# Row sums of squares of four SSD blocks made earlier, and the last head pair's loads re-ordered, in a hybrid attention and SSD layer

## The chip, the cores and the metric

The kernel runs on one core of a Trainium2 chip. The time is that of one execution in device microseconds. The kernel before took 2189.46 us, the median of three runs from 2188.48 to 2193.33 us.

## The reference

For 2048 tokens of width 1024 the layer computes a projection, two branches, and one output product.

```
proj = x @ w_in                                   # q, k, v, z_att, z_ssm, xbc, dt
o_d, l_d = dilated_window_attention(q, k, v)      # for dilation d = 1, 4, 16; l_d is the log of the exponentials' sum
y_att = sum_d softmax_d(l_d) * o_d                # 16 heads of 64
y_att = rms_norm(y_att * silu(z_att))
y = ssd_chunked(conv_silu(xbc), dt, ...) + d_skip * xs
y_ssm = rms_norm(y * silu(z_ssm))
out = concat(y_att, y_ssm) @ w_out
x = layer_norm(alpha * x + out)
```

`rms_norm(u)` divides each token's row of 1024 by the root of its mean square. The kernel multiplies the un-normed rows by `w_out` (the gain is folded into the weight) and scales the product by the reciprocal root afterwards, so the sum of squares of a row is needed only when its product is added to the result.

## The kernel before

Everything is fp32, but large products are made of three float32r products: high times high, high times low, low times high. The program has three stretches.

**Projections and SSD.** `proj` makes 52 column tiles of the projection, each of 96 products of 128x512 (L111 to L113). While the last 20 tiles run, `ssd(n, g)` works on 16 blocks n of 128 tokens and two groups g of heads. It writes `y * silu(z)` of a block, its operand for the output product, to DRAM as `d_us` and, for the first four blocks, also split into high and low as `d_uh`. The order in this stretch is made by a scheduler from its own estimates.

**Attention.** Eight pairs of heads, pr = 0 to 7, one after the other. A pair has 24 steps `(d, qd, half)`: dilation 0 to 2, four quarters, two halves. In each step TensorE makes the scores (L528), DVE adds the bias table and takes a minimum (L536), ACT makes the exponentials (L544), TensorE transposes them (L557), DVE copies them out (L559) and TensorE multiplies them by v (L577) two to three steps later. From here on the order on TensorE, DVE, ACT and POOL is the order in which the code is written; only the order on SP, which issues most DMAs, is the scheduler's.

When the last step of a pair is done, its minima and sums (`st`) are transposed, written to DRAM (`d_st`, L605), read back in another layout (`cm`, L611), turned into the softmax weights over the three dilations (`weights`, L618 to L628), written (`d_wd`, L629) and read back broadcast over partitions (`wb`, six loads of 512 KB, L642). `combine` then weights and sums the three dilations' results `num` and multiplies by `silu(z)`. For pairs 0 to 6 this runs on POOL during the next pair, `weights` at the steps (0,3,0) and (0,3,1), `combine` at (1,0,0), (1,1,0), (1,3,0) and (2,2,0), and the result goes to DRAM as `d_ua` (L660). For pair 7 there is no next pair: it runs on DVE within the output stretch, its three `num` are first multiplied by `silu(z)` (`gate`, L782), and its result stays on the chip in four tiles, here called `u7` (L649).

**Output.** `product(n, br)` makes 48 products of 128x512 for block n and branch br (1 is SSD, 0 is attention): two halves `hf` of 24, each over eight weight tiles e with three products. The order is (0,1) (1,1) (2,1) (3,1), then (0,0) (1,0) (2,0) (3,0), then both branches of each block from 4 on. The operand is split by ACT (L707) and DVE (L708); for the SSD branch of blocks 0 to 3 the split is loaded from `d_uh` instead (`fetch_parts`). The eight weight tiles of the SSD branch, W[8] to W[15], are loaded by POOL during pair 7 into tiles that attention has done with, those of the attention branch, W[0] to W[7], in the output stretch, as `num`, `qp`, `v` and `wb` come free.

The sum of squares: `fetch_raw` loads the unsplit operand, `squares` squares it (ACT, L712) and sums over the eight slices (DVE `TENSOR_REDUCE`, L714), and TensorE sums over partitions by a product with a column of ones (L743), which stands in TensorE's order **between the two halves of the same block's product**. `add` takes the reciprocal root (L750, L751) and adds the scaled product to the result (L755).

The prediction's steps are in `ssd` (from L340), `weights` and `combine` (L613, L631), `fetch_parts` (L684) to `add` (L747), `gate` (L780) and the two loops from L790.

Of the kernel before, what the change touches and what calls it, by code (L numbers as in the profile page):

```python
# [9 lines left out]
F32 = mybir.dt.float32  # L10
F32R = mybir.dt.float32r
AF = mybir.ActivationFunctionType
# [16 lines left out]
def hybrid_layer(ctx, tc, xT, xc, w52, wv, convw, convb, dtb, alog, dskp, gcol, wout,  # L29
# [37 lines left out]
    nc.gpsimd.memset(epst, EPS)  # L67
    gc = consts.tile([128, 16], F32, name="gc")
    def evac(i, o, a):
        if i % 2:  # L70
            nc.vector.tensor_copy(o, a)
        else:
            nc.scalar.copy(o, a)


    with ExitStack() as c1:
# [263 lines left out]
        def ssd(n, g):  # L340
# [71 lines left out]
            if n < 4:  # L412
# [4 lines left out]
                for p, t in enumerate((yh, yl)):  # L417
                    nc.sync.dma_start(d_uh[g][n][:, p], v4(t.bitcast(F32)))

        units = [(n, g) for n in range(16) for g in range(2)]  # L420
        jobs = []
# [17 lines left out]
    with ExitStack() as c2:  # L439
# [251 lines left out]

        def fetch_raw(n, br):
            u = raw[n, br] = row().rearrange("p (c t) -> p c t", t=128)
            if br:
                for g in range(2):
                    (nc.gpsimd if n < 2 else nc.sync).dma_start(u[:, 4 * g:4 * g + 4], d_us[g][n])
            else:
                nc.sync.dma_start(u[:, 0:7], d_ua[n])
# [10 lines left out]

        def squares(n, br):  # L710
            u = raw.pop((n, br))
# [8 lines left out]

        raw, sr = {}, {}
        UT = ["num", "num", "qp"]
        banks = [("S", psS), ("S", psS), ("S", psS), ("S", psS), ("T", psT), ("T", psT)]

        def product(n, br):
# [4 lines left out]
            for hf in range(2):  # L730
# [9 lines left out]
                pss.append(ps)  # L740
                if hf == 0:
                    pn = psN.tile([128, 512], F32, name="N")
                    nc.tensor.matmul(pn[:, 0:1], sr.pop((n, br)), one, start=True, stop=True)  # L743
            free.append(t)
            return pss, pn

        def add(n, br, pss, pn):  # L747

            r = small[:, 8 * n + br:8 * n + br + 1]
            nc.scalar.activation(r, pn[:, 0:1], AF.Sqrt, bias=epst, scale=1.0 / D)  # L750
            nc.vector.reciprocal(r, r)  # L751
# [27 lines left out]

        def gate(d, eng):  # L780
            num = f2(pairs[7]["num"][d])
            eng.tensor_tensor(num, num, zt7, op=OP.mult)  # L782

# [6 lines left out]
        with tc.manual_schedule(engines={E.PE, E.DVE, E.Activation, E.Pool}):  # L790
            for i in range(len(todo) + TA + 1):
# [16 lines left out]
                if i > TA:  # L808
# [7 lines left out]
                    at = d, qd, half  # L816
                    if pr and at in ((0, 3, 0), (0, 3, 1)):
                        weights(pairs[pr - 1], half)
                    step = ((1, 0, 0), (1, 1, 0), (1, 3, 0), (2, 2, 0))
                    if pr and at in step:  # L820
                        combine(pairs[pr - 1], step.index(at))
                    if pr < 7:
# [4 lines left out]
                        if (qd, half) == (3, 1) and d < 2:  # L827
                            load_dil(pairs[pr + 1], d)
                    elif at == (1, 0, 0):
                        for e, name in ((8, "kh_0"), (9, "kl_0"), (10, "qh"), (11, "ql"), (12, "v")):  # L830
                            load_w(e, name)
                    elif at == (1, 1, 0):
                        zt7 = big("num", F32)
                        nc.gpsimd.dma_start(zt7, d_za[7])
                    elif at == (1, 3, 0):
                        for e, name in ((13, "qp"), (14, "qp")):
                            load_w(e, name)
                        fetch_parts(0, 1)
                        gate(0, nc.gpsimd)
                    elif at == (1, 3, 1):  # L840
                        load_w(15, "v")
                    elif at == (2, 2, 0):
                        fetch_parts(1, 1)
                    if pr and at == (0, 3, 1):
                        load_dil(pairs[pr], 2)
            A = pairs[7]
            small = stp.tile([128, 192], F32, name="st")
            os_ += [big("kh_1", F32), big("kl_1", F32)]
            fetch_raw(0, 1)
            squares(0, 1)  # L850
            residual(0)
            fetch_raw(1, 1)
            residual(1)
            fetch_parts(2, 1)
            fetch_raw(2, 1)
            order = [(n, 1) for n in range(4)] + [(n, 0) for n in range(4)]
            order += [(n, br) for n in range(4, 16) for br in (1, 0)]
            for i, (n, br) in enumerate(order):
                ps = product(n, br)
                if i == 0:  # L860
                    weights(A, 0)
                    weights(A, 1)
                    gate(1, nc.vector)
                    gate(2, nc.vector)
                if i == 1:
                    fetch_parts(3, 1)
                    fetch_raw(3, 1)
                    for d in range(3):
# [9 lines left out]
                if 2 <= i < len(order) - 2:  # L878
                    fetch_parts(*order[i + 2])
                    fetch_raw(*order[i + 2])  # L880
                    if order[i + 2][1] and order[i + 2][0] >= 4:
                        residual(order[i + 2][0])
                if i + 1 < len(order):
# [5 lines left out]
                if i == 2:  # L889
                    split(0, 0, slice(0, 7))  # L890
                add(n, br, *ps)
                if br == 0:
# [69 lines left out]
```

## Time and profile before

| | |
|---|---|
| median of three runs | 2189.46 us |
| profiled execution | 2193.83 us, of it 2192.0 us span |
| TensorE busy | 2138.5 us, 98% |
| DVE, ACT, POOL busy | 53%, 39%, 38% |
| granted TensorE clock, mean | 0.984 of full speed |
| chain that ended last | TensorE 89%, DMA 4%, DVE 4%, ACT 2% |

TensorE is busy nearly all the time. The profile's slices of 54.8 us show where it is not: the first slice, then two slices (33 and 34, about 1754 to 1863 us) with 7 and 6 tenths, and the last. The two slices in the middle are the passage from attention to the output stretch. In the same two slices the granted clock shows 8 tenths, and the DMA engines move 360 and 276 GB/s, among the most in the program. In such a kernel an edit changes the time if it changes what TensorE does, or how long it stands still at those places.

### The profile page before, as it was taken

The numbers are of one execution on the slowest core, as the hardware profiler recorded it, in microseconds if no ns is written. First come the engines' busy times: TensorE is split into PE (matmuls) and PEld (weight loads), VectorE is DVE, ScalarE is ACT, GpSimd is POOL, SyncE is SP. The second block draws the span as 40 slices with busy tenths as digits, with TensorE's granted clock in tenths as the row PEclk, the third lists the DMA queues.
The fourth block names the chain that finished last, engine by engine and source line by source line (L and its number), as shares of the span: only waits on it lengthen the run. The fifth ranks groups of instructions, "written<-read, shape, count | busy, mean of one in ns | idle before, by whom it ended". The sixth has DMA issues, their size and how long they took to land.

```text
span 2192.0 us, 37071 instructions
## 1 busy us (share of the span) xinstructions
PE 2138.5 (98%) x13968; PEld 1784.6 (81%) x13968; DVE 1166.2 (53%) x2941; ACT 847.8 (39%) x2289; POOL 838.8 (38%) x589
## 2 busy tenths in 40 slices
PE   8999999999999999999999999999999976999998
PEld 8999888888888888888888878888878865888886
DVE  4000255555223555554544258888888845655655
ACT  4101122223112333232345368887888841222221
POOL 3101010102442455555555321776666670322322
PEclk9999999999999999999999979999999988999999
DMA  8644222224786656555543542777876799232220
GB/s 281 182 133 139 70 78 71 77 71 148 249 262 208 206 194 198 178 190 177 171 157 129 195 148 76 228 219 223 241 216 184 208 360 276 99 104 83 93 84 29
DMA packets 213955, 363.66 MB, mean 166 GB/s; under 512 B 37776, under 2 KB 125968, under 8 KB 203536
## 3 DMA queue, kind: packets, MB, share of 16 engines
q1 hardware_dynamic: 197408, 278.45, 41.8%
q0 software_dynamic: 16368, 82.84, 10.6%
q8 instruction: 110, 1.80, 0.3%
q14 instruction: 69, 0.57, 0.1%
HBM read 226.62 MB, written 134.61 MB: 165 GB/s over the span
## 4 chain that ended last, share of the span: by engine, by line
PE 89%; DMA 4%; DVE 4%; ACT 2%; SPq 1%; issue 1%; POOL 0%; DVEq 0%; POOLq 0%; ACTq 0%
PE pp L112 14%; PE pp L111 14%; PE pp L113 14%; PE N L577 6%; PE T L557 6%; PE S L528 6%; PE S L737 3%; PE S L739 3%; PE S L738 3%; PE pp L155 2%; PE pp L156 2%; PE pp L154 2%; PE T L737 2%; PE T L738 2%; PE T L739 2%; PE ss L386 1%
## 5 line engine op out<-in xcount | busy, mean ns | idle before, releaser
L111 PE MATMUL pp<-xh,whi 128*128 128x512 f32 x1408 | 550.3, 391 | 0.0
L112 PE MATMUL pp<-xl,whi 128*128 128x512 f32 x1408 | 549.6, 390 | 0.0
L113 PE MATMUL pp<-xh,wlo 128*128 128x512 f32 x1408 | 548.5, 390 | 0.0
L544 ACT ACTIVATE P<-P,st 128x256 f32<-128x256 f32 (+1 forms) x768 | 345.4, 452 | 94.7 <-DVE st L536 94.1
L113 PEld LDWEIGHTS pp<-xh,wlo 128*128 128x128 f32 x1408 | 264.3, 188 | 55.4
L111 PEld LDWEIGHTS pp<-xh,whi 128*128 128x128 f32 x1408 | 264.4, 188 | 54.7
L112 PEld LDWEIGHTS pp<-xl,whi 128*128 128x128 f32 x1408 | 264.4, 188 | 54.0
L536 DVE CUSTOM_DVE_ANT_0 P<-S,tb 128x256 f32<-128x256 f32 (+1 forms) x768 | 235.3, 362 | 107.3 <-PE S L528 76.1
L101 POOL TENSOR_TENSOR wlo<-wraw,whi 128x1024 fp32r<-128x1024 f32 x44 | 105.5, 2397 | 365.1 <-ACT whi L100 352.1
L559 DVE COPY PT<-T 128x512 f32<-128x512 f32 (+1 forms) x304 | 196.5, 677 | 2.3 <-PE T L557 2.2
L557 PE MATMUL T<-ident,P 128*128 128x128 f32 x1200 | 179.4, 286 | 6.3 <-DVE PT L559 5.9
L577 PE MATMUL N<-PT,v 128*64 128x128 f32 x2400 | 176.4, 284 | 0.0
L577 PEld LDWEIGHTS N<-PT,v 128*64 128x64 f32 x2400 | 129.2, 138 | 33.2 <-issue 22.6
L557 PEld LDWEIGHTS T<-ident,P 128*128 128x128 f32 x1200 | 129.7, 142 | 31.5 <-DVE PT L559 7.3
L544 ACT ACTIVATION_READ_ACCUMULATOR P<-P,st 128x1 f32 x768 | 144.7, 188 | 0.0
L644 POOL TENSOR_TENSOR wb<-num,wb 128x2048 f32<-128x2048 f32 x21 | 96.3, 4586 | 97.1 <-DMA wb<-d_wd 69.3
L528 PE MATMUL S<-kh,qp 64*128 64x256 f32 (+1 forms) x1024 | 126.3, 306 | 0.0
L379 DVE TENSOR_SCALAR mt<-csb,cs 128x128 f32<-128x128 f32 x256 | 75.2, 363 | 71.2 <-DMA csb<-d_cs 71.2
L714 DVE TENSOR_REDUCE tb<-P 128x128 f32<-128x1024 f32 x32 | 64.0, 2000 | 85.6 <-PE N L743 49.2
L528 PEld LDWEIGHTS S<-kh,qp 64*128 64x128 f32 x1024 | 88.8, 188 | 22.0 <-issue 20.9
L154 PE MATMUL pp<-vh,xh 128*128 128x384 f32 (+1 forms) x304 | 95.0, 320 | 6.0 <-ACT xh L184 5.4
L100 ACT CAST whi<-wraw 128x1024 fp32r<-128x1024 f32 x44 | 46.1, 1047 | 138.3 <-PE pp L112 130.5
(295 smaller groups left out, 3807.1 us busy)
## 6 DMA issues: line engine op xcount, KB each, us to landing
v<-d_v POOLq DMA_DIRECT2D x24, 1024.0 KB, 7.0
wb<-d_wd SPq DMA_DIRECT2D x48, 512.0 KB
wraw<-w SPq DMA_DIRECT2D x44, 512.0 KB
d_wo<-wot SPq DMA_DIRECT2D x32, 512.0 KB
csb<-d_cs SPq DMA_DIRECT2D x32, 512.0 KB
d_v<-vt SPq DMA_DIRECT2D x64, 192.0 KB
d_za<-ev SPq DMA_DIRECT2D x32, 256.0 KB
d_xs<-cvo SPq DMA_DIRECT2D x8, 1024.0 KB
```

What stands on the lines that cost most here:

```text
L111: nc.tensor.matmul(ps, hi[:, k, :], h, start=(k == 0), stop=False)
L112: nc.tensor.matmul(ps, hi[:, k, :], l, start=False, stop=False)
L113: nc.tensor.matmul(ps, lo[:, k, :], h, start=False, stop=(k == 7))
L154: nc.tensor.matmul(ps, h, vw[k][0], start=(k == 0), stop=False)
L528: nc.tensor.matmul(ov(sp[h][:, 256 * b:256 * b + w]), A["q"][d][x][hr, blk], kv(A["k"][y][hr]), start=(m == 0), stop=(m == 2))
L536: nc.vector.tensor_tensor_reduce(P[:, h, b, 256 - w:256], sp[h][:, c0:c0 + w], tab[:, h, tab.shape[2] - w:], 1.0, 3.0e38, OP.add, OP.min, ...
L544: nc.scalar.activation(p, p, AF.Exp, bias=stat(A, 0, d, h, blk), scale=-1.0, accum_out=stat(A, 1, d, h, blk))
L557: nc.tensor.transpose(tp[:, h, b], P[:, h, b, 128 * which:128 * which + 128], ident)
L559: nc.vector.tensor_copy(pt[:, :, bl[0]:2], tp[:, :, bl[0]:2])
L577: nc.tensor.matmul(nm[64 * h:64 * h + 64, bq * 128:bq * 128 + 128], v[:, k, 64 * h:64 * h + 64], pts[which][:, h, b], start=(f or not whic ...
L737: nc.tensor.matmul(ps, uh[:, e, :], wh, start=(e == 0), stop=False)
L738: nc.tensor.matmul(ps, uh[:, e, :], wl, start=False, stop=False)
```

## The change

Three parts. (1) `ssd` squares the finished operand of blocks 0 to 3 on POOL, sums over its four slices on DVE and over partitions on TensorE, and keeps the sums of both groups in a small tile `ssq`; the output stretch takes one root and one reciprocal of all four columns, and the SSD products of blocks 0 to 3 have no raw load, no squares and no product with ones any more. (2) The loads of pair 7 stand in one function, `last_pair`, at other steps: W[8] and W[9] at (0,0,0), the parts of block 0 at (1,1,0), those of block 1 at (1,3,1), the gate's `silu(z)` at (2,2,0). The gate's product for dilation 0 moves from POOL to DVE, beside the other two. The parts of block 2 are loaded after the first product, into the tile of block 0. (3) For all pairs `weights` stands one half-step earlier, at (0,2,1) and (0,3,0).

```diff
@@ ssd
+                nc.gpsimd.tensor_tensor(xd, y, y, op=OP.mult)
+                nc.vector.tensor_reduce(cbm, xd.rearrange("p c l -> p l c"), axis=mybir.AxisListType.X, op=OP.add)
+                pq = ss.tile([128, 512], F32, name="ss")
+                nc.tensor.matmul(pq[:, 0:1], cbm, one, start=True, stop=True)
+                if g:
+                    nc.vector.tensor_tensor(ssq[:, n:n + 1], pq[:, 0:1], ssq[:, n:n + 1], op=OP.add)
+                else:
+                    nc.vector.tensor_copy(ssq[:, n:n + 1], pq[:, 0:1])
@@ fetch_raw and squares
+            if br and n < 4:
+                return
...
@@ product
-                if hf == 0:
+                if hf == 0 and (n, br) in sr:
                     pn = psN.tile([128, 512], F32, name="N")
                     nc.tensor.matmul(pn[:, 0:1], sr.pop((n, br)), one, start=True, stop=True)
...
@@ add
+            if len(pss) == 3:
+                r = small[:, 8 * n + br:8 * n + br + 1]
+                nc.scalar.activation(r, pss.pop(1)[:, 0:1], AF.Sqrt, bias=epst, scale=1.0 / D)
+                nc.vector.reciprocal(r, r)
+            else:
+                r = ssq[:, n:n + 1]
@@ new
+        def last_pair(at):
+
+            if at == (0, 0, 0):
+                load_w(8, "kh_0")
+                load_w(9, "kl_0")
+            elif at == (1, 0, 0):
+                load_w(10, "qh")
+                load_w(11, "ql")
+                load_w(12, "v")
+            elif at == (1, 1, 0):
+                fetch_parts(0, 1)
+            elif at == (1, 3, 0):
+                load_w(13, "qp")
+                load_w(14, "qp")
+            elif at == (1, 3, 1):
+                load_w(15, "v")
+                fetch_parts(1, 1)
+            elif at == (2, 2, 0):
+                z7.append(big("num", F32))
+                nc.gpsimd.dma_start(z7[0], d_za[7])
@@ the attention loop
-                    if pr and at in ((0, 3, 0), (0, 3, 1)):
-                        weights(pairs[pr - 1], half)
+                    if pr and at in ((0, 2, 1), (0, 3, 0)):
+                        weights(pairs[pr - 1], qd - 2)
...
-                    elif at == (1, 0, 0):
-                        for e, name in ((8, "kh_0"), (9, "kl_0"), (10, "qh"), (11, "ql"), (12, "v")):
-                            load_w(e, name)
-                    elif at == (1, 1, 0):
-                        zt7 = big("num", F32)
-                        nc.gpsimd.dma_start(zt7, d_za[7])
-                    elif at == (1, 3, 0):
-                        for e, name in ((13, "qp"), (14, "qp")):
-                            load_w(e, name)
-                        fetch_parts(0, 1)
-                        gate(0, nc.gpsimd)
-                    elif at == (1, 3, 1):
-                        load_w(15, "v")
-                    elif at == (2, 2, 0):
-                        fetch_parts(1, 1)
@@ before the output loop
-            fetch_raw(0, 1)
-            squares(0, 1)
-            residual(0)
-            fetch_raw(1, 1)
-            residual(1)
-            fetch_parts(2, 1)
-            fetch_raw(2, 1)
@@ the output loop
-                    gate(1, nc.vector)
-                    gate(2, nc.vector)
+                    nc.scalar.activation(ssq, ssq, AF.Sqrt, bias=epst, scale=1.0 / D)
+                    nc.vector.reciprocal(ssq, ssq)
+                    residual(0)
+                    residual(1)
+                    fetch_parts(2, 1)
+                    for num in A["num"]:
+                        nc.vector.tensor_tensor(f2(num), f2(num), z7[0], op=OP.mult)
```

The change also moves instructions on the engines. On POOL, in the second half of pair 7 and at its end, this stood before (`d_uh0` and `d_uh1` are the two groups' parts, `num_18141` the tile for block 0 and `num_18434` that for block 1; L782 is the gate, L659 the last step of pair 6's `combine`):

```order
L689 DMA num_18141<-d_uh0_113 128x2x512
L689 DMA num_18141<-d_uh1_114 128x2x512
L782 TENSOR_TENSOR num_17537<-num_17537,num_17946 128x2048
L675 DMA v_18198<-d_wo_115 128x2048
L659 TENSOR_TENSOR wb_18431<-wb_18132,wb_18429 128x16x16x8
L689 DMA num_18434<-d_uh0_113 128x2x512
L689 DMA num_18434<-d_uh1_114 128x2x512
L696 DMA P_18505<-d_us0_111 128x512
L696 DMA P_18505<-d_us1_112 128x512
L718 DMA kh_18503<-xc 128x1024
```

And this stands there now (L699 is the load of parts, L663 and L669 are steps of pair 6's `combine`, L817 loads the gate's `silu(z)`):

```order
L699 DMA num_17987<-d_uh0_113 128x2x512
L699 DMA num_17987<-d_uh1_114 128x2x512
L654 TENSOR_TENSOR wb_18174<-num_17200,wb_18174 128x2048
L663 TENSOR_TENSOR wb_18174<-wb_18174,wb_17982 128x2048
L685 DMA qp_18179<-d_wo_115 128x2048
L685 DMA qp_18181<-d_wo_115 128x2048
L685 DMA v_18236<-d_wo_115 128x2048
L699 DMA num_18238<-d_uh0_113 128x2x512
L699 DMA num_18238<-d_uh1_114 128x2x512
L669 TENSOR_TENSOR wb_18472<-wb_18174,wb_18470 128x16x16x8
L817 DMA num_18475<-d_za7_99 128x2048
L732 DMA kh_18543<-xc 128x1024 x2
```

The gate is gone from in front of pair 6's last combining step, the parts of blocks 0 and 1 stand ahead of it, and no raw operand is loaded behind it. On SP, at the end of pair 7, this stood before:

```order
L718 DMA kl<-xc 128x1024 x2
L696 DMA P<-d_us_111 128x512
L696 DMA P<-d_us_112 128x512
L605 DMA d_st_124<-sT 16x16x8 x4
L660 DMA d_ua<-wb 128x16x128
L611 DMA cm<-d_st_124 128x6x32
```

And this stands there now, with the two rows that follow it:

```order
L732 DMA kl<-xc 128x1024 x2
L615 DMA d_st_124<-sT 16x16x8 x4
L670 DMA d_ua<-wb 128x16x128
L621 DMA cm<-d_st_124 128x6x32
L710 DMA P<-d_ua 128x896 x3
L639 DMA d_wd_132<-cm 128x3x32
L652 DMA wb<-d_wd_132 64x2048 x6
```

The raw loads ahead of `d_st` are gone, and three loads of the attention branch's operand, of which the first stood behind the `wb` loads, now stand ahead of `d_wd`. One pair earlier, at the end of pair 6, the write of `d_ua` stood behind `cm`; now it stands inside the four `d_st` writes:

```order
L615 DMA d_st_123<-sT 16x16x8 x3
L670 DMA d_ua<-wb 128x16x128
L615 DMA d_st_123<-sT 16x16x8
L621 DMA cm<-d_st_123 128x6x32
L639 DMA d_wd_131<-cm 128x3x32
```

The same stands at one other pair's end; at the other pairs `d_ua` is still behind `cm`. On DVE, in the output stretch, the three gates (L884) now follow the weights, and between the last combining step (L659) and the first part of block 0's attention operand (L720) one addition is left, where two reductions stood as well:

```order
L638 TENSOR_TENSOR cm<-cm,mm 128x3x32
L879 RECIPROCAL ssq<-ssq 128x4
L884 TENSOR_TENSOR num<-num 128x2048 x3
L773 SCALAR_TENSOR_TENSOR kh<-S,ssq,kh 128x512 x2
L654 TENSOR_TENSOR wb<-num,wb 128x2048 x2
L663 TENSOR_TENSOR wb<-wb 128x2048
L654 TENSOR_TENSOR wb<-num,wb 128x2048
L659 TENSOR_TENSOR PT<-wb 128x16x4x8 x4
L773 SCALAR_TENSOR_TENSOR kh<-S,ssq,kh 128x512 x2
L720 TENSOR_TENSOR num<-P,num 128x896
```

## Rows read from the trace of the kernel before

**Rows 1.** Waits of TensorE: engine, line, releaser, us in total, times, longest.

```profile
PE N L743 <- DVE tb L714: 23.7, 2, 19.2
PE S L737 <- DMA num<-d_uh: 7.0, 1, 7.0
```

**Rows 2.** Windows: us, busy of PE, PEld, DVE, ACT, POOL, clock, DMA share, GB/s.

```profile
1779.50:1845.20 65.70, 35.01 (x128) 27.37 (x126) 25.12 (x25) 11.68 (x15) 18.31 (x23) 0.76 1.02 279
1845.00:1865.00 20.00, 19.85 (x76) 16.09 (x77) 9.23 (x14) 1.88 (x4) 0.00 (x0) 0.85 0.91 343
```

**Rows 3.** Chain of waits after pair 7's last step: start us, us, what.

```profile
1781.75 11.66 DMA d_st<-sT
...
1793.49 11.46 DMA cm<-d_st
...
1807.45 3.21 DMA d_wd<-cm
...
1814.25 24.14 DMA wb<-d_wd
...
1838.49 2.30 DVE wb L644
...
1841.42 1.89 DVE PT L649 x3
...
1843.31 1.79 DVE tb L714
...
1845.15 0.58 PE N L743 x2
```

**Rows 4.** TensorE timeline: start us, us, line, operation, count, [idle before].

```profile
1786.74 0.79 PE L737 MATMUL S<-kh,num 128*128 128x512 f32 x1 [6.96 <-DMA num<-d_uh]
...
1870.15 0.40 PE L738 MATMUL S<-wb,num 128*128 128x512 f32 x1
...
1870.38 0.39 PE L739 MATMUL S<-wb,num 128*128 128x512 f32 x1
...
1870.62 0.28 PE L743 MATMUL N<-one,tb 128*128 128x1 f32 x2
```

**Rows 5.** POOL timeline at pair 7's end and at the last weight loads.

```profile
1776.40 4.54 POOL L782 TENSOR_TENSOR num<-num 128x2048 f32<-128x2048 f32 x1
...
1781.52 4.51 POOL L659 TENSOR_TENSOR wb<-wb 128x2048 f32<-128x2048 f32 x1
...
1841.29 0.53 POOL L675 DMA_DIRECT2D num<-d_wo  x1 [7.23 <-issue]
...
1843.61 0.54 POOL L675 DMA_DIRECT2D wb<-d_wo  x1 [0.19 <-issue]
```

**Rows 6.** SP timeline: end of pair 5 (first two rows) and of pair 7.

```profile
1658.47 1.80 SPq L605 DMA_DIRECT2D d_st<-sT  x4
...
1663.65 0.38 SPq L611 DMA_DIRECT2D cm<-d_st  x1
...
1786.05 0.38 SPq L660 DMA_DIRECT2D d_ua<-wb  x1
...
1799.91 1.18 SPq L696 DMA_DIRECT2D P<-d_us  x1
```

**Rows 7.** Line L675, the sixteen weight loads of both branches: time to landing.

```profile
DMA to landing us min/median/max: 5.0/11.3/17.8
```

**Rows 8.** DVE: `weights` after pair 5, the subtraction of a split, and line L755.

```profile
1671.88 0.18 DVE L618 TENSOR_TENSOR mm<-cm 128x32 f32<-128x32 f32 x1
...
1848.37 1.08 DVE L708 TENSOR_TENSOR num<-P,num 128x896 fp32r<-128x896 f32 x1
...
L755 DVE SCALAR_TENSOR_TENSOR kh<-S,st,kh x22: 741/750/751, 1813.8 to 2137.5; 128x512 f32<-128x512 f32 x22
```

**Rows 9.** Groups by line in SSD, 820 to 960 us: busy us, mean ns.

```profile
L401 POOL TENSOR_TENSOR y<-y,zt 128x512 f32<-128x512 f32 x8 | 13.1, 1634 | 4.1 <-DVE y L400 4.0
...
L400 DVE TENSOR_TENSOR y<-ss,xd 128x512 f32<-128x512 f32 x8 | 5.5, 688 | 3.7 <-POOL xd L399 3.7
```

More of the change, by code (lines that the diff above doesn't have):

```diff
@@ L68, in hybrid_layer @@
     gc = consts.tile([128, 16], F32, name="gc")
+    ssq = consts.tile([128, 4], F32, name="ssq")
     def evac(i, o, a):
@@ L695, in fetch_raw @@
                 for g in range(2):
-                    (nc.gpsimd if n < 2 else nc.sync).dma_start(u[:, 4 * g:4 * g + 4], d_us[g][n])
+                    nc.sync.dma_start(u[:, 4 * g:4 * g + 4], d_us[g][n])
             else:
@@ L710, in squares @@
         def squares(n, br):
+            if br and n < 4:
+                return
             u = raw.pop((n, br))
@@ L719, in residual @@
             nc.scalar.activation(o, o, AF.Copy, scale=ALPHA)
-        raw, sr = {}, {}
+        raw, sr, z7 = {}, {}, []
         UT = ["num", "num", "qp"]
@@ L740, in product, with add @@
                 pss.append(ps)
-                if hf == 0:
+                if hf == 0 and (n, br) in sr:
                     pn = psN.tile([128, 512], F32, name="N")
                     nc.tensor.matmul(pn[:, 0:1], sr.pop((n, br)), one, start=True, stop=True)
+                    pss.append(pn)
             free.append(t)
[L745 to L751, printed above, removed]
+            return pss
+        def add(n, br, pss):
+            if len(pss) == 3:
[4 more added lines that the diff above has]
+                r = ssq[:, n:n + 1]
             o = O[n]
@@ L778, in norm @@
             nc.sync.dma_start(rows, o)
-        def gate(d, eng):
-            num = f2(pairs[7]["num"][d])
-            eng.tensor_tensor(num, num, zt7, op=OP.mult)
+        def last_pair(at):
[17 more added lines that the diff above has]
+                nc.gpsimd.dma_start(z7[0], d_za[7])
         O = {}
@@ L828, in hybrid_layer @@
                             load_dil(pairs[pr + 1], d)
-                    elif at == (1, 0, 0):
-                        for e, name in ((8, "kh_0"), (9, "kl_0"), (10, "qh"), (11, "ql"), (12, "v")):
-                            load_w(e, name)
-                    elif at == (1, 1, 0):
-                        zt7 = big("num", F32)
-                        nc.gpsimd.dma_start(zt7, d_za[7])
-                    elif at == (1, 3, 0):
-                        for e, name in ((13, "qp"), (14, "qp")):
-                            load_w(e, name)
-                        fetch_parts(0, 1)
-                        gate(0, nc.gpsimd)
-                    elif at == (1, 3, 1):
-                        load_w(15, "v")
-                    elif at == (2, 2, 0):
-                        fetch_parts(1, 1)
                     if pr and at == (0, 3, 1):
                         load_dil(pairs[pr], 2)
+                    if pr == 7:
+                        last_pair(at)
             A = pairs[7]
@@ L862, in hybrid_layer @@
                     weights(A, 1)
-                    gate(1, nc.vector)
-                    gate(2, nc.vector)
+                    nc.scalar.activation(ssq, ssq, AF.Sqrt, bias=epst, scale=1.0 / D)
[5 more added lines that the diff above has]
+                        nc.vector.tensor_tensor(f2(num), f2(num), z7[0], op=OP.mult)
                 if i == 1:
                     fetch_parts(3, 1)
-                    fetch_raw(3, 1)
                     for d in range(3):
@@ L880, in hybrid_layer @@
                     fetch_raw(*order[i + 2])
-                    if order[i + 2][1] and order[i + 2][0] >= 4:
-                        residual(order[i + 2][0])
                 if i + 1 < len(order):
@@ L890, in hybrid_layer @@
                     split(0, 0, slice(0, 7))
-                add(n, br, *ps)
+                if 2 <= i < len(order) - 2 and order[i + 2][1]:
+                    residual(order[i + 2][0])
+                add(n, br, ps)
                 if br == 0:
```

## The prediction

> **What bounds the kernel now.** I read the waits of TensorE first, since it is busy 98% of the span: two entries matter, 23.7 us for DVE's sums of squares in two waits, and 7.0 us for the parts of block 0 [rows 1]. The windows place them: in the 65.7 us from the end of attention to 1845.2 TensorE works 35.0 us, at 0.76 of its clock [rows 2]. It idles before the first product [rows 4], before the first product with ones, and 19.2 us in the third block, whose reduction stands on DVE behind pair 7's combining [rows 1, 3].
>
> The chain of waits says what the combining itself waits for [rows 3]. The last statistics are written (11.66 us), gathered (11.46), the weights made, written (3.21) and read back as `wb` (24.14 for the last), and DVE combines. `u7` is complete at 1843.3. This chain passes through no TensorE product. So two things hold the output stretch: TensorE waits for sums that it could do without, and the block after the fourth, (0,0), needs `u7`, whoever is ready for it.
>
> **What the waits that go are worth.** Four SSD products are 192 matmuls. Two that follow each other start 0.23 us apart [rows 4], so they take 45 us. Attention's last TensorE work ends 7.0 us before 1786.74, at 1779.8 [rows 4]. With the parts of block 0 issued half a pair earlier and no sum needed in between, the four products end near 1825. Then TensorE stands still until (0,0) can start. The 30.7 us of idle time in rows 1 are thus not the gain; most of them come back as one wait for `u7`. The gain is what happens after `u7`, and how much earlier `u7` comes.
>
> **After `u7`.** Before, 72 matmuls were still to be done after `u7` ahead of (0,0): half of block 2 and block 3. The mark is the product with ones of (0,0), after its first 24 matmuls: it stands at 1870.6 [rows 4], 27.3 us after `u7`. Now DVE's path from `u7` is one addition of two halves, 0.75 us each, and a subtraction of 1.08 us [rows 8], so the first matmul of (0,0) can start 2.6 us after `u7`. It then meets the next late thing, the attention branch's weights. POOL issues the last five of eight from 1841.29 to 1843.61 [rows 5], and the slowest landed 17.8 us after its issue [rows 7]: 1861.4, or 18.1 us after `u7`. Before, TensorE came to it later than that. In that time two loads of the attention operand (128x896 fp32, 0.46 MB each) ran too; by the new order on SP they are over earlier. At the 343 GB/s of that window [rows 2] they are 0.92 MB, 2.7 us. So I take the last weight at `u7` + 15.4, and three matmuls behind it at half clock, 0.46 us each, 1.4: the mark at `u7` + 16.8 instead of 27.3, a gain of **10.5 us**. Without the relief it is 7.8; if the weights were no bound, 24 matmuls at half clock after 2.6 us give `u7` + 13.6, a gain of 13.7.
>
> **How much earlier `u7` comes.** In a quiet pair the statistics are written 5.2 us after their first issue, and `cm` is used 8.2 us after its own [rows 6, 8], together 13.4 at most; here the two transfers take 23.2 from the last issue on [rows 3], since POOL's loads run beside them. Three edits touch it. The gate's 4.54 us stood in front of pair 6's last combining step [rows 5]; without it the write of `d_ua`, which `cm` follows in SP's order, is issued right after `d_st` near 1782.2 instead of 1786.05 [rows 3, 6]: 3.8 us. Two raw loads (128x512, 0.52 MB) leave the queue ahead of `d_st`: at 343 GB/s 1.5 us. Against it, three operand loads (1.38 MB, 4.0 us at that rate) now stand ahead of `d_wd`; the weights take 2.5 us from the gather's end to the issue of `d_wd` [rows 3], so 1.5 us show. The gate's three products on DVE lie under the `wb` loads (24 us). Sum: **3.8 us** earlier. The ends are -1.5 (only the loads ahead of `d_wd` count) and 9.8 (as quiet as pair 5).
>
> POOL has a new wait: the parts of block 2 go into block 0's tile, so its load stands behind TensorE's first product, until about 1791, and behind it on POOL stand the parts of block 3 and the weight loads. Block 2's product is due at 1802. A late load there costs nothing as long as it is under the 17 us in which TensorE now waits for `u7`; if `u7` came that much earlier it would cost its whole lateness.
>
> The Trainium skill, page "DMA: Bandwidth & Descriptors", section "Queues, rings and completion order", speaks against the 3.8: each DMA engine takes turns between the queues, a packet of each at a time, so SP's small pieces advance by POOL's packets whatever is taken out of SP's own queue. Rows 3 and 6 agree in that the same write takes twice as long beside loads; no row shows the turns. By it, since POOL now issues the gate's 1 MB and two residual loads in this stretch, `u7` would gain nothing; this is the first rival.
>
> **What SSD costs.** There TensorE is the bound, so its eight added products with ones count: 0.28 us per pair of passes at full clock [rows 4], **2.2 us**. The ends are 0 (they fit into gaps) and 4.6 (0.58 each, the row at half clock [rows 3]). The squares (POOL) and reductions (DVE) lie beside it. From the last sum to the product with ones the chain is 0.69 for the addition, 1.63 for POOL's gate product, the same again for the square [rows 9], and about 1.0 for a reduction half as long as the 1.79 one [rows 3]: 5.0 us. TensorE's written order has 34 to 60 projection matmuls in between, 7.8 to 13.8 us, which covers it. If that cover were gone, it would be up to 5 us in each of eight units.
>
> **`weights` a half-step earlier.** From pair 5's first `d_st` to pair 7's last are 123.3 us [rows 6, 3] for 48 steps: 2.6 us a step. DVE used `cm` 8.2 us after its issue without waiting [rows 6, 8], so 5.6 us remain. The nearest row for a small transfer is `d_wd`, 3.21 us [rows 3], so it is in time. At two of seven ends the 1 MB write of `d_ua` now stands ahead of `cm`: at 343 GB/s 3.1 us, against a margin of 2.4. I take 1 us of stall of DVE, and so of TensorE behind it, at each: **2 us**. The ends are 0 and 6.
>
> **The sum.** 10.5 + 3.8 - 2.2 - 2.0 = 10.1 us less. The profiled execution took 2193.8 us, 4.4 above the median of the three runs, 2189.5. From 2193.8 this gives 2183.7, and from the median about 2179, which I predict.
>
> **The rivals.** (1) *The chain is not shortened and the weights come as late as before.* For it: DMA is at a busy share of 1.02 over the whole passage [rows 2], and bytes are moved more than removed. Against it: the gate's place on POOL is plain. 7.8 - 1.5 - 4.2 = 2.1 less: 2187. (2) *The chain runs as in a quiet pair.* For it: 2 MB of weights, two raw rows and the gate's place leave this stretch. Against it: the gate's load and the residuals come into it. 10.5 + 9.8 - 4.2 = 16.1 less: 2173. (3) *Slower: `cm` is late in every pair.* The place is DVE's first `weights` instruction, at which the exponentials and the copies for TensorE queue up. With 5.6 us left, a `cm` that lands 8.1 us after its issue stalls 2.5 us in each of seven pairs, 17 us, which takes back more than the 14.3 of the two gains: the point from which it decides. At the 11.46 us of the crowded end [rows 3] it would be 5.9 us, 41 us in all: about 2217. Against it: the seven earlier ends are quiet, and DVE never waited there.
>
> **How the numbers follow.** Forecast 0.50, rival 1 0.22, rival 2 0.20, rival 3 with other stalls 0.08. About 0.2%, 4.4 us, is what a measurement can tell from no change. The forecast's lower end and part of rival 1 fall within it, so faster 0.72, within 0.2% 0.18, slower 0.10. The range runs from rival 2 with unbound weights (19.3 less) to rival 1 with the stalls at their dear ends: 2169 to 2189. The forecast's own range is 2174 to 2184.
>
> **What would show it.** Right: no wait of TensorE for parts or sums between attention and (0,0); four products on end from about 1780; one wait of some 17 us before (0,0); `u7` near 1839.5 (in this trace's times, plus 2 to 4 us from SSD and attention); within the first half of (0,0) short waits for weights; the mark 10 to 15 us earlier. Wrong: `cm` as late as now after its issue (the 3.8), waits of TensorE for the squares in SSD (the 2.2), waits of DVE for `cm` at more than two ends (the 2), or waits for weights that push the mark beyond `u7` + 20.

## The result: slower by 0.27%, and the profile after

The changed kernel took 2194.8 us (median of 19 runs) against 2190.87 us of the kernel before (19 runs); the ratio is 1.0027, 95% interval 1.0015 to 1.0038. Forecast were 2179 us and a range up to 2189. The profiled executions lie closer together, with spans of 2192.2 and 2192.0 us, because the one of before (2193.83 us) was 3.0 us above its median and the one of after (2194.01) 0.8 below. So the two traces differ by 0.2 us where the medians differ by 3.9; what the rest is, no trace shows.

DVE, ACT, POOL and SP are VectorE, ScalarE, GpSimd and SyncE; PE is TensorE, PEld its weight loads. First TensorE's waits, as in [rows 1]: engine, line, releaser, us in total, times, longest.

```profile
PE N L587 <- DVE PT L569: 11.8, 7, 8.3
PE S L751 <- issue: 10.5, 1, 10.5
PE S L751 <- DMA wb<-d_wo: 4.2, 2, 2.7
PE S L751 <- DMA v<-d_wo: 3.6, 1, 3.6
```

The 30.7 us of before are gone, and one wait of 10.5 us in front of (0,0) has come, with short ones for weights behind it. But the first line is new and does not belong to the output stretch: L587 is the product of probabilities and values in attention, and it stood 8.3 us for one copy by DVE. TensorE's timeline in pair 7 (start us, us, instruction, [idle before]) has it here:

```profile
1749.46 1.12 PE L587 MATMUL N<-PT,v 128*64 128x128 f32 x8 [8.27 <-DVE PT L569]
```

DVE's timeline of the same kernel, just before:

```profile
1747.25 0.19 DVE L628 TENSOR_TENSOR mm<-cm 128x32 f32<-128x32 f32 x1 [9.05 <-DMA cm<-d_st]
```

And POOL's, with the two weight loads that now stand at (0,0,0):

```profile
1733.19 0.59 POOL L685 DMA_DIRECT2D kh<-d_wo  x1
1733.78 0.54 POOL L685 DMA_DIRECT2D kl<-d_wo  x1
```

DVE stands at the first instruction of `weights` and waits for `cm`; the copy for TensorE is queued behind it. SP's timeline at the end of pair 6, of the kernel before:

```profile
1720.97 2.21 SPq L605 DMA_DIRECT2D d_st<-sT  x4
1727.96 0.38 SPq L611 DMA_DIRECT2D cm<-d_st  x1
1728.38 0.54 SPq L660 DMA_DIRECT2D d_ua<-wb  x1
```

The same end in the kernel after:

```profile
1726.81 1.31 SPq L615 DMA_DIRECT2D d_st<-sT  x3
1728.81 0.38 SPq L670 DMA_DIRECT2D d_ua<-wb  x1
1729.23 3.28 SPq L615 DMA_DIRECT2D d_st<-sT  x1
1735.19 0.38 SPq L621 DMA_DIRECT2D cm<-d_st  x1
```

Before, `cm` was issued ahead of the 1 MB write of d_ua and used 6.4 us later without a wait. After, d_ua stands ahead of the last statistics and of `cm`, so that `cm` is issued 2.0 us behind the first of the weight loads (2 MB), and it is used 12.1 us after its issue. By then d_ua is no longer in its way. The DMA queues of the kernel after show it, q1 with SP's transfers and q0 with POOL's (packets, MB, share of the 16 engines), from 1732 to 1733, 1734 to 1735, 1741 to 1742, 1742 to 1743 and 1744.0 to 1744.5 us:

```profile
q1 hardware_dynamic: 575, 0.29, 104.7%
...
q0 software_dynamic: 12, 0.10, 77.7%
q1 hardware_dynamic: 45, 0.01, 5.6%
...
q0 software_dynamic: 71, 0.29, 94.4%
q1 hardware_dynamic: 73, 0.01, 7.7%
...
q0 software_dynamic: 69, 0.28, 95.5%
q1 hardware_dynamic: 67, 0.01, 6.8%
...
q1 hardware_dynamic: 344, 0.04, 58.9%
q0 software_dynamic: 16, 0.03, 21.9%
```

The write of d_ua is all but done by 1734, before `cm` is issued at 1735.19. The first packets of `cm`, which is 768 packets of 128 bytes, move at 1739.5; what holds them until then is open. Then it moves about one packet for each 4 KB packet of POOL's loads, and 344 packets in half a us once these run out. So d_ua made `cm` late, and beside the loads it was slow.

TensorE's clock then falls too (windows: us, busy of PE, PEld, DVE, ACT, POOL, clock, DMA share, GB/s; the wait, what follows it, and the 65.7 us from attention's end, which answer to the first window of [rows 2]):

```profile
1737.50:1749.50 12.00, 3.73 (x46) 2.81 (x42) 2.88 (x16) 3.12 (x15) 0.00 (x0) 0.84 0.62 203
1749.50:1760.00 10.50, 10.50 (x92) 8.41 (x94) 9.04 (x42) 8.41 (x32) 0.00 (x0) 0.70 0.66 137
1795.50:1861.20 65.70, 50.98 (x210) 39.77 (x209) 30.08 (x34) 9.65 (x13) 7.11 (x12) 0.92 0.97 301
```

From pair 6's last statistics to pair 7's (ACT's copies of `sT`) it took 59.4 us before and takes 69.4 now. The passage behind attention went the other way: TensorE works 51 of 65.7 us instead of 35, at a clock of 0.92 instead of 0.76. Its chain of waits, which answers to [rows 3] (start us, us, what):

```profile
1798.19 11.08 DMA d_st<-sT
1809.42 6.04 DMA cm<-d_st
...
1817.97 8.11 DMA d_wd<-cm
...
1829.37 14.47 DMA wb<-d_wd
...
1850.38 17.19 DMA wb<-d_wo
```

`cm` and `wb` come faster, d_wd slower (8.11 us, behind the three loads of d_ua rows). DVE's timeline has the last additions of `u7`:

```profile
1847.58 2.50 DVE L659 TENSOR_TENSOR PT<-wb 128x512 f32<-128x512 f32 x4
```

TensorE's has the product with ones of (0,0), the mark of the prediction [rows 4]:

```profile
1869.12 0.42 PE L757 MATMUL N<-one,tb 128*128 128x1 f32 x2
```

The account of the two traces, after minus before: the projection's last product is 4.2 us later, the first pair's end another 2.0, pairs 1 to 6 together 0.4 quicker, pair 7 10.0 slower; from attention's end to `u7` it is 9.0 less (54.2 instead of 63.2), from there to the mark 8.3 less (19.0 instead of 27.3), and from the mark to the end 1.7 more. Sum: 0.2.

### The profile page after: what moved, and what is told of

Read it like the earlier page. It is cut to its first block, busy times and chain, and to the rows that moved or that the text cites. A ratio compares the mean times of both kernels' runs of the same rounds, so it can differ in the third digit from the quotient of the medians.

```text
span 2192.2 us, 37099 instructions
## 1 busy us (share of the span) xinstructions
PE 2142.8 (98%) x13976; PEld 1788.8 (82%) x13976; DVE 1166.7 (53%) x2951; ACT 843.4 (38%) x2282; POOL 835.9 (38%) x592
## 4 chain that ended last, share of the span: by engine, by line
PE 84%; DMA 8%; DVE 3%; POOL 2%; issue 1%; SPq 1%; ACT 1%; POOLq 0%; DVEq 0%; ACTq 0%
PE pp L114 14%; PE pp L113 14%; PE pp L112 14%; PE S L538 6%; PE N L587 5%; PE T L567 5%; PE S L751 3%; PE S L753 3%; PE S L752 3%; PE pp L156 2%; PE pp L157 2%; PE pp L155 2%; PE T L751 2%; PE T L753 2%; PE T L752 2%; PE ss L397 1%
## 5 line engine op out<-in xcount | busy, mean ns | idle before, releaser
L114 PEld LDWEIGHTS pp<-xh,wlo 128*128 128x128 f32 x1408 | 264.8, 188 | 55.4
L587 PE MATMUL N<-PT,v 128*64 128x128 f32 x2400 | 178.1, 286 | 11.9 <-DVE PT L569 11.8
L587 PEld LDWEIGHTS N<-PT,v 128*64 128x64 f32 x2400 | 130.4, 139 | 46.0 <-issue 22.4
L538 PEld LDWEIGHTS S<-kh,qp 64*128 64x128 f32 x1024 | 90.3, 191 | 22.5 <-issue 21.3
L156 PE MATMUL pp<-vl,xh 128*128 128x384 f32 (+1 forms) x304 | 96.8, 320 | 0.1
L157 PE MATMUL pp<-vh,xl 128*128 128x384 f32 (+1 forms) x304 | 96.2, 319 | 0.0
```

The lines of the kernel that those rows point to most:

```text
L114: nc.tensor.matmul(ps, lo[:, k, :], h, start=False, stop=(k == 7))
L156: nc.tensor.matmul(ps, h, vw[k][1], start=False, stop=False)
L157: nc.tensor.matmul(ps, l, vw[k][0], start=False, stop=(k == 7))
L538: nc.tensor.matmul(ov(sp[h][:, 256 * b:256 * b + w]), A["q"][d][x][hr, blk], kv(A["k"][y][hr]), start=(m == 0), stop=(m == 2))
L587: nc.tensor.matmul(nm[64 * h:64 * h + 64, bq * 128:bq * 128 + 128], v[:, k, 64 * h:64 * h + 64], pts[which][:, h, b], start=(f or not whic ...
```

## The experiments

Theory A: the loss is pair 7's wait for `cm`, and its cause the earlier `weights`. Theory B: its cause is the two weight loads beside it. Theory C: the loss lies in SSD. "Both undone" below is the changed kernel with `weights` and these loads back in their old places.

**Two by two: `weights` back, loads back, both.**

```
-  if pr and at in ((0, 2, 1), (0, 3, 0)):
-      weights(pairs[pr - 1], qd - 2)
+  if pr and at in ((0, 3, 0), (0, 3, 1)):
+      weights(pairs[pr - 1], half)
```
```
-  if at == (0, 0, 0):
+  if at == (1, 0, 0):
       load_w(8, "kh_0")
       load_w(9, "kl_0")
-  elif at == (1, 0, 0):
       load_w(10, "qh")
```

> The changed kernel with pair p-1's `weights` back at steps (0,3,0) and (0,3,1); all else stays. Theory A (the half-step is the loss): pair 7 ended 15.8 us later than before, the seven earlier ends 5.0 to 7.4, so about 10 us are lost in pair 7, where DVE waited 9.05 us for `cm`. They come back: attention's end near 1786, no wait of DVE for `cm` in the pairs, time about 2194.8 - 10 = 2185. Theory B (the two weight loads now at (0,0,0) slow `cm` to 12 us after its issue): half of that remains, since the later place gives only 2.6 us a half-step more: about 2190. Theory C (the loss lies ahead of attention, in SSD): no change, 2195.

> The changed kernel with the loads of weights 8 and 9 back at (1,0,0); `weights` stays a half-step earlier. Theory A (the half-step, and the 1 MB write of d_ua that now stands ahead of `cm` on SP): DVE still waits some 6 to 9 us for `cm` in pair 7, time 2192 to 2195. Theory B (the loads): `cm` lands some 7 us after its issue, the stall shrinks from 9 to about 3 us, attention ends 6 us earlier: about 2188. Theory C: 2195.

> The changed kernel with both undone: `weights` at (0,3,0), (0,3,1) and the loads of weights 8 and 9 at (1,0,0). Theory A: as with `weights` alone, 2185, perhaps a microsecond less. Theory B: all of the stall goes only here: 2185, against 2188 to 2190 with one of the two. Theory C: 2195.

Measured: 2190.13 us (ratio to before 1.0001, 0.9991 to 1.0012), 2191.21 (1.0000, 0.9992 to 1.0009) and 2188.34 (0.9989, 0.9981 to 0.9998). Attention ended at 1784.9, 1787.8 and 1783.8 us, against 1795.9. Neither A nor B alone holds: with the loads away, DVE's wait in pair 7 is 2.91 us instead of 9.05 (line below), with `weights` back it is nothing, though the loads are there.

```profile
1740.50 0.19 DVE L628 TENSOR_TENSOR mm<-cm 128x32 f32<-128x32 f32 x1 [2.91 <-DMA cm<-d_st]
```

There `cm` is issued at 1734.44 and used 6.1 us later, half of the 12.1 beside the loads. With `weights` back it is issued at 1732.76, ahead of d_ua and of the loads.

The 8 to 12 us by which attention ends earlier brought only 3.6 to 6.5 in the time, by the medians. Putting `weights` back gave 11.0 at attention's end, but `u7` came 61.3 us after it instead of 54.2. The edit had also changed SP's order at the end of pair 7, which is the scheduler's. SP's timeline with `weights` back:

```profile
1785.16 0.82 SPq L615 DMA_DIRECT2D d_st<-sT  x2
1791.79 0.38 SPq L670 DMA_DIRECT2D d_ua<-wb  x1
1792.22 8.85 SPq L615 DMA_DIRECT2D d_st<-sT  x2
1807.34 0.37 SPq L621 DMA_DIRECT2D cm<-d_st  x1
```

d_ua waits for POOL's last combining step of pair 6, which ended 6.9 us behind attention's end here and 2.1 us ahead of it in the changed kernel. The last statistics stand behind d_ua, and `cm` is issued 22.5 us after attention's end instead of 13.5. With the loads back, d_ua stands ahead of all four pieces and `cm` is issued 21.1 us after it; with both back the order is that of the changed kernel (14.6). So the first two runs are not clean in the time; DVE's waits in pair 7 lie ahead of this.

**d_ua off SP's queue.** In the changed kernel and with the loads back `cm` stood behind d_ua. This edit leaves the early `weights` and the early loads:

```
-  nc.sync.dma_start(dap(d_ua, pr * 128, [[7 * 128, 128], [128 * 7 * 128, 16], [1, 128]]),
+  nc.gpsimd.dma_start(dap(d_ua, pr * 128, [[7 * 128, 128], [128 * 7 * 128, 16], [1, 128]]),
```

> The changed kernel with the writes of d_ua issued by POOL, behind the product that makes their data, instead of by SP. `weights` stays early and the loads of weights 8 and 9 stay at (0,0,0); on SP nothing stands between d_st and `cm` any more. If the place of d_ua on SP is what makes `cm` late in pair 7, DVE's wait of 9.05 us shrinks below 3 us and the time is about 2188. If the bytes are (the 1 MB of d_ua and the 2 MB of weights run beside `cm` either way), `cm` still lands 10 us or more after its issue, the wait stays at 5 us or more, and the time is 2191 to 2195.

Measured: 2184.72 us, ratio 0.9963 (0.9950 to 0.9977), 10 us under the changed kernel, more than expected. SP's timeline of this run at the end of pair 6:

```profile
1722.15 1.93 SPq L615 DMA_DIRECT2D d_st<-sT  x4
1727.32 0.38 SPq L621 DMA_DIRECT2D cm<-d_st  x1
```

And DVE's:

```profile
1733.49 0.18 DVE L628 TENSOR_TENSOR mm<-cm 128x32 f32<-128x32 f32 x1
```

`cm` is used 6.2 us after its issue and nobody waits. It is issued 3.0 us ahead of the weight loads, not behind them; POOL's first of the two, and SP's queue from 1730 to 1731 us, in which the whole of `cm` passes:

```profile
1730.29 0.56 POOL L685 DMA_DIRECT2D kh<-d_wo  x1
...
q1 hardware_dynamic: 784, 0.10, 63.3%
```

So the place of d_ua on SP is what it takes, and the loads, once `cm` comes behind them, made a wait of some 3 us one of 9. Attention ends at 1780.6, as before, though its first pair ended 4.7 us later: with `cm` in time the early `weights` is worth 0.6 us a pair (62.5 us before, 61.9 here).

**`weights` a half-step earlier alone, in the kernel before** (the first edit above, the other way round):

> The kernel before with one edit: `weights` a half-step earlier, at (0,2,1) and (0,3,0). The loads of weights 8 and 9 stay at (1,0,0); the order on SP then has d_ua ahead of the last d_st piece and `cm` at the ends of pairs 2 and 6. Theory A1 (the half-step alone costs several us where d_ua stands ahead of `cm`): DVE waits 2 to 4 us for `cm` at these two ends, as in the run with only the loads put back (6.7 us of waits of TensorE for DVE), less 0.6 us in each other pair: attention ends 1 to 4 us later than 1780.1. My term was 2 us of loss. Theory B1 (only the loads beside it make `cm` late): no wait, attention ends some 3 us earlier. By the time: A1 2192 to 2195, B1 2189 to 2191, before 2191.5.

Measured: 2192.26 us, ratio 0.9999 (0.9990 to 1.0008); attention ends at 1780.7. DVE's waits at the two ends where d_ua stands ahead:

```profile
1484.02 0.19 DVE L618 TENSOR_TENSOR mm<-cm 128x32 f32<-128x32 f32 x1 [1.48 <-DMA cm<-d_st]
1733.59 0.19 DVE L618 TENSOR_TENSOR mm<-cm 128x32 f32<-128x32 f32 x1 [1.72 <-DMA cm<-d_st]
```

1.5 and 1.7 us, where 2 to 4 were expected and my prediction had 1 each. The term was about right for this edit by itself. What it lacked is the changed loads beside it.

**Without the sums in SSD** (the four sums are the constant 1):

```
-  nc.gpsimd.tensor_tensor(xd, y, y, op=OP.mult)
-  nc.vector.tensor_reduce(cbm, xd.rearrange("p c l -> p l c"), axis=mybir.AxisListType.X, op=OP.add)
-  pq = ss.tile([128, 512], F32, name="ss")
-  nc.tensor.matmul(pq[:, 0:1], cbm, one, start=True, stop=True)
-  if g:
...
```

> The changed kernel without the sums of squares in SSD (their eight squares, reductions, products with ones and additions are left out; the four sums are the constant 1). My sum's term: 2.2 us less, 2192.6. By the trace after, the projection ends 4.24 us later than before (2.25 of it from about 550 us, ahead of the first SSD unit) and attention another 2 us later: if all of it hangs on the sums, 4 to 6 us less, 2189 to 2191, with the last projection product at 1266 and the first pair's end at 1345.5. Theory C (the sums are the whole loss): below 2187.

Measured: 2193.78 us, ratio 1.0012 (1.0003 to 1.0021), 1.0 less than the changed kernel by the medians and 0.15% by the ratios. C falls. The last projection product comes at 1267.35; over the four profiles without the sums it is 1266.5 to 1267.8 (mean 1267.1), over the ten with them 1268.3 to 1271.0 (mean 1269.7): 2.6 us, and the 4.2 of the first trace is its upper end. The expected 1345.5 for the first pair was missed: it ended at 1347.6.

**The sums alone, in the kernel before** (the SSD part and the missing raw rows, squares and products with ones of blocks 0 to 3; gate, loads and `weights` as before):

> The kernel before with the first part of the change alone: the four sums made in SSD, and no raw loads, squares and products with ones for the first four blocks behind attention. Gate, loads and `weights` stay where they were. My reading: SSD ends about 2 us later; the 23.7 us of waits for the sums of squares go, and come back as one wait for `u7` in front of (0,0) of 15 to 20 us; `u7` stays within 3 us of 1843.3 and the product with ones of (0,0) comes 17 to 19 us after it instead of 27.3. Net 4 to 8 us less: 2184 to 2188. If the sums cost more in SSD than they give (rival): 2191 or more.

Measured: 2186.06 us, ratio 0.9979 (0.9963 to 0.9995), as expected. Two details were not. The wait in front of (0,0) is 4.5 us, not 15 to 20, since the first product waited 5.5 us for its parts. And `u7` comes 55.4 us after attention's end, 7.8 less than before, though neither gate nor loads moved. The chain shows where from:

```profile
1789.86 7.64 DMA d_st<-sT
1797.64 12.53 DMA cm<-d_st
1812.67 2.50 DMA d_wd<-cm
1818.44 14.50 DMA wb<-d_wd
```

`wb` takes 14.50 us instead of 24.14 [rows 3]. The edit took eight raw loads (0.26 MB each) out of this passage. They were issued from 1777.7 to 1802 us, and the trace has no landing of one more than 9.8 us after its issue, so they were about over when `wb` began (1810.7). Beside `wb` 4.1 MB moved in all (1815 to 1833 us) instead of 6.7 (1811 to 1838.4 us before), at 225 and 244 GB/s. How the raw loads lead to that is not shown. From attention's end to the mark 15.8 of the changed kernel's 17.3 us are there with the sums alone; the version with both undone, which has the gate's removal and the spread loads on top, is at 0.9989 (0.9981 to 0.9998), so the runs show no gain from these.

**What bounds the passage: two loads out of the way.** Both on the version with both undone. First, the d_ua rows of blocks 0 to 2 go to POOL, block 0's behind the second weight load and the others behind the last; then, weight loads 4 and 5 go ahead of 0 to 3:

```
-  nc.sync.dma_start(u[:, 0:7], d_ua[n])
+  (nc.gpsimd if n < 3 else nc.sync).dma_start(u[:, 0:7], d_ua[n])
...
       load_w(e, name)
+      if e == 1:
+          fetch_raw(0, 0)
```
```
-  for e, name in enumerate(("num", "num", "num", "num", "qp", "v", "wb", "wb")):
+  load_w(4, "qp")
+  load_w(5, "v")
+  for e, name in ((0, "num"), (1, "num"), (2, "num"), (3, "num"), (6, "wb"), (7, "wb")):
       load_w(e, name)
```

> The version with both undone (`weights` back, loads of weights 8 and 9 back; 2188.3), and the three loads of d_ua rows for blocks 0 to 2 moved from SP, where they stand between `cm` and d_wd, to POOL: block 0's between the attention branch's loads 1 and 2, the others behind load 7. If the three loads ahead of it are what made d_wd 6.58 us long there (3.21 before), it becomes 3 to 4 us, `wb` is issued some 3 us earlier, `u7` is complete at about 1838.5 instead of 1841.6, time about 2185. If the passage is bound by the bytes alone, `wb` takes so much longer that `u7` stays within 1 us, time 2188.

> The version with both undone (2188.3) with the attention branch's loads 4 and 5, whose tiles are free early, issued ahead of loads 0 to 3, at about 1814 instead of 1840. Five loads remain behind `u7` there, now three. If only the queue behind `u7` counts, the last weight lands 17.3 x 3/5 = 10.4 us after its issue instead of 17.3, and the product with ones of (0,0) comes up to 6 us earlier: 2183. If the whole passage is bound by its bytes, the 2 MB slow `wb` and `u7` by what the end gains: 2187 to 2189.

Measured: 2186.97 us (0.9976, 0.9966 to 0.9987) and 2184.71 (0.9968, 0.9956 to 0.9981). In the first, d_wd takes 2.65 us instead of 6.58, as expected, but `u7` is only 1.0 us earlier after attention's end (56.7 instead of 57.7). In the second, `u7` is 5.5 us later after attention's end, and the mark 1.9 us earlier. Its chain of waits:

```profile
1819.64 25.02 DMA wb<-d_wd
...
1849.87 10.43 DMA wb<-d_wo
```

The 10.43 us for the last weight came as expected, paid for by 25.02 us for `wb`. In these two edits bytes taken from one transfer were given to the next, to within 1 to 2 us. That only the number of bytes counts is not shown: the next two runs move transfers too, and one gains more. The time of the second, 3.6 us under its parent, is more than the 2 us the traces explain.

**d_ua on POOL's queue in the kernel before, and in the changed one with the loads back:**

> The kernel before with one edit: the writes of d_ua issued by POOL, behind the product that makes their data. In the kernel before `cm` went ahead of d_ua at the seven early ends, so nothing stalls there and nothing is to be had; at pair 7's end SP stood 3.7 us at d_ua (1782.3 to 1786.05) with `cm` behind it. If the 10 us that the same edit took off the changed kernel were the stall of pair 7, this gives 0 to 4 us: 2188 to 2192. If d_ua on SP costs something of its own everywhere, it gives the same 10: 2182.

> The changed kernel with the writes of d_ua issued by POOL (2184.7) and the loads of weights 8 and 9 back at (1,0,0). If only the two together made `cm` late, nothing is left to win by moving the loads: attention ends within 1 us of where it did (1780.6), and 2 MB more fall into the busy stretch behind: 2184 to 2187. If the loads still cost beside `cm`, 2181 to 2183.

Measured: 2185.82 us (0.9982, 0.9965 to 0.9998) and 2182.31 (0.9961, 0.9948 to 0.9975). The first is just below its expected 2188 to 2192, so the edit has a worth of its own: the pairs do not change (attention ends at 1780.2), but `u7` comes at 1833.6 instead of 1843.3, mostly because `wb` takes 17.66 us instead of 24.14; beside it 4.8 MB moved in all instead of 6.7, at 233 and 244 GB/s. Why fewer is open. The second is 2.4 us under the same kernel with the early loads (2184.72), in the range given for loads that still cost beside `cm` (2181 to 2183), but not by that way: attention ends at 1779.9, 0.7 us earlier, and the pairs take the same time. The intervals overlap. `u7` is 57.0 us after attention's end instead of 59.4. Why 2 MB loaded later should help is open.

**Three edits that helped, together** (d_ua on POOL, the d_ua rows late, loads 4 and 5 first, on the changed kernel):

> The changed kernel with the writes of d_ua issued by POOL (2184.7), the loads of d_ua rows for blocks 0 to 2 moved to POOL behind the attention branch's loads, and that branch's loads 4 and 5 issued ahead of 0 to 3. Singly the last two took 1.4 and 3.6 us off the version with both undone. If they add up: 2180 to 2182. If the passage behind attention is bound by its bytes, they share one gain: 2182 to 2185.

Measured: 2179.83 us, ratio 0.9949 (0.9934 to 0.9965): faster than both kernels, and just below the 2180 to 2182 of gains that add up. The mark stands at 1856.0, right behind the last weight, and `wb` and that weight still hold it:

```profile
1813.14 20.09 DMA wb<-d_wd
1838.47 16.44 DMA wb<-d_wo
```

## Why the prediction was wrong

**The step that failed: "At two of seven ends the 1 MB write of d_ua now stands ahead of `cm`: at 343 GB/s 3.1 us, against a margin of 2.4. I take 1 us of stall of DVE ... at each: 2 us."** Both ends were named rightly, and by itself the edit costs 1.5 and 1.7 us there. In the changed kernel they are 2.72 and 9.05 us. The price took d_ua to run alone; the same change puts 2 MB of weights on POOL at (0,0,0) of pair 7, beside `cm`, and I counted these loads only as bytes that leave the last passage. The runs showed instead that d_ua on SP delays the issue of `cm` until those loads are under way, and that `cm` beside them takes 12.1 us to its use, against 6.1 without them. Pair 7 became 10.0 us longer, with 9.05 of DVE's wait in it and a clock of 0.70 behind it. A price for `cm` beside POOL's loads stood in [rows 3], 11.46 us against the 12.1 measured; I used it in rival 3 alone and took the 3.21 of d_wd here. The upper bound of 6 was too low for the same reason. The range's upper end was also added up wrongly: rival 1 with stalls of 6 us is 7.8 - 1.5 - 2.2 - 6.0, or 1.9 us slower, 2191 and not 2189. In the traces the terms came out as 8.3 + 9.0 - 4.2 - 9.6 (pairs 1 to 7), less 2.0 (first pair) and 1.7 (behind the mark) that had no term: 0.2 us slower.

**After `u7`: 10.5, measured 8.3**, within its bounds (7.8 to 13.7); and the late weights are the bound, as said. Not in the sum: after the waits for them TensorE runs on at nearly half clock, the lower of its two levels (1.2 of 2.4 GHz), beyond the mark, and from the mark to the end it takes 1.7 us more. Of these, 1.3 lie between the mark and the same product of the next block (12.6 us at a clock of 0.89, instead of 11.4 at 1.00). The window around the mark:

```profile
1861.20:1872.00 10.80, 6.56 (x17) 4.56 (x16) 2.58 (x4) 1.32 (x2) 0.00 (x0) 0.53 0.55 215
```

**`u7` earlier: 3.8, measured 9.0**, within -1.5 to 9.8, but with the wrong cause. I gave 3.8 to the gate's place on POOL and cancelled the rest. That place gave nothing: `cm` was issued 13.5 us after attention's end, against 13.4 before, and 10 with the sums alone, where the gate's product is still on POOL. The sums alone gave 7.8: I had counted two of the eight raw loads, those ahead of d_st, and not the six issued behind them, at 1787 to 1802 us, beside d_st and `cm`. The three d_ua rows ahead of d_wd made it 8.11 us instead of 3.21, but moving them away brought `u7` forward by only 1.0, near the 1.5 I gave.

**SSD: 2.2, measured 2.6**, right; in the trace after it was 4.2. At the first pair's end the ten profiles with the sums are 3.8 us behind the four without, on the mean, so part of the next loss goes with them. Nothing of the reductions or squares was waited for. **The start of attention** had no term. From the last projection product to the first pair's end it was 2.0 us slower in the trace and 1.1 to 2.1 in all runs but two; in the two that have neither the sums nor the new output stretch it was 0.2 to 0.3. The clock from 1290 to 1350 us was 0.93 before and 0.87 after; why is open.

**The rivals.** Rival 3 had the right mechanism, `cm` late in front of DVE's `weights`, at the wrong places: it assumed seven ends, and it was two, one of them dear. I gave it 0.08 because the ends were quiet before; they were so in the kernel before, and one of them was no longer. Rival 1 fell: the chain did get shorter, by 9.0 us. But the turns between queues that stood behind it are there: the gather moved 73 and 67 packets in two us beside 71 and 69 of POOL's queue. The Trainium skill, "DMA: Bandwidth & Descriptors", "Queues, rings and completion order", states such turns, a packet of each queue at a time, and the trace agrees. I had applied the turns behind attention only, and not at the end of pair 6, where 768 small packets met the weight loads. Behind attention I overlooked that four of the eight raw loads left POOL's own queue.

**Which part did what, by the times:** the sums alone 0.21% faster; the early `weights` alone nothing (0.9999); gate and spread loads no gain that can be told; `weights` and two loads together, with d_ua ahead of `cm`, 6.5 us slower by the medians (0.38% by the ratios).

## What to carry over

When one part of a change brings a wait closer to its deadline and another part moves transfers, price the wait with the moved transfers beside it: here the one alone made a wait of 1.7 to 2.9 us, the other none, both together 9. Look in the new order at what stands ahead of a small, urgent transfer in its own queue; moving the large one to another queue (one line) was worth 10 us in the changed kernel and 6 in the one before, by the medians. A large transfer ahead can cost not by its bytes but by delaying the small one until others are under way: look at when it is issued. Look at that order in each experiment too, where a scheduler makes it. In a passage whose DMA engines are busy throughout, shortening one transfer of the chain may only lengthen the next one.

## What the runs showed of the hardware

- A stall of TensorE cost more than its length: pair 7 took 69.4 us with a wait of 8.27 us and 58.8 with d_ua off SP's queue and no such wait. Behind the wait the granted clock was 0.70 over 10.5 us, and 1.00 over the same stretch without it (1733.5 to 1745 us of that run); it was 0.53 over the 10.8 us that hold the waits for the last weights, where 1 would be 2.4 GHz.
- In one stretch two DMA queues moved about packet for packet, though the sizes differed 32-fold: the 96 KB gather moved 73 and 67 packets of 128 bytes in two us beside 71 and 69 packets of 4 KB, and 344 in half a us when the other queue had nearly run dry. It was used 12.1 us after its issue behind 2 MB of loads, and 6.2 us after it when issued 3.0 us ahead of them.
- The 3 MB read of `wb` was as slow as the bytes beside it were many: 6.7, 4.8 and 4.1 MB in all moved in 27.4, 20.6 and 18.0 us (the kernel before, the same with d_ua on POOL, the sums alone), at 244, 233 and 225 GB/s.
- A projection stretch of the same code ended between 1268.3 and 1271.0 us over ten profiles, so 2 us at such a place need more than one trace.
